# HGRN2's scan: TensorE's work of a head in four groups instead of thirteen steps

## The chip, the core and the metric

The kernel runs on one core of a Trainium2 chip. The metric is the device time of one execution in microseconds (us). A core has five engines that matter here: TensorE (PE; its weight loads are listed as PEld), VectorE (DVE), ScalarE (ACT), GpSimd (POOL) and SyncE (SP, which issues DMAs). Each takes its own queue in order, and semaphores tie the queues together.

## What is computed

One inference step of a decoder with two layers on 512 prompt tokens and 64 sample tokens (8 sequences of 8). The change lies in layer 0's token mixer, HGRN2, a gated linear recurrence with 8 heads of size 128:

```python
q, fz, v, g = jnp.split(x @ w_in, 4, axis=-1)
f = lbf + (1.0 - lbf) * jax.nn.sigmoid(fz)
qh = heads(jax.nn.silu(q) * HG_QK_SCALE)
kh = heads(1.0 - f)
# per token: S_t = diag(f_t) S_{t-1} + k_t v_t^T,  o_t = S_t^T q_t   (computed in chunks)
o, s = hgrn2_chunk_scan(qh, kh, heads(v), heads(jnp.log(f)), s0)
o = rms_norm(o, gnorm_w) * jax.nn.silu(heads(g))
return o.reshape(bsz, t, D_MODEL) @ w_out, s
```

The samples start from a given state per sequence and head, the prompt from zero. Output, new prompt state and new sample states are all results.

## The kernel before

The program is written out by hand: every engine's queue holds its instructions in the order in which the code issues them, and no scheduler moves them. The HGRN2 stage goes head by head. `proj(h)` is a generator that issues the projections of head h and yields after each unit, a unit being three TensorE matmuls into the same output (the activations and the weights are each split into a high and a low part; lines L299 to L301). A head has 16 units for the forget gate f, 16 for q and 16 for the output gate g, each 16 made of 8 with 320 columns and 8 with 256. An even head has 40 units of 256 columns for V ahead of them, for itself and the next head. So an even projection has 88 units and an odd one 48.

Behind each 16 units a side generator is queued, and each unit issues one step of the oldest: `decay` (from f: e, L, k and the four running sums b, on ACT and DVE), `factors` (KH, QH, KL, QL, K2, E2 and the load of the sample states S0) and `queries` (silu of q and g on ACT, tile qg, then QH, QL and Q2 on DVE; it waits QWAIT = 9 steps first).

`scan(h)` is head h's recurrence, a generator whose steps are issued between the units of `proj(h+1)`, at the unit numbers of `SCAN_AT` (the first tuple where the projection is of an even head, the second where it is odd; a step stands behind the unit of its number, the first being number 0). A step ends at each `yield`. What TensorE does in the steps: transposes of K2 (L661, L668), the states (L674 for the prompt, L688 for the samples), the scores of four blocks of 128 tokens (L704, L709, one step per block), products of the samples' queries with their states (L719), the samples' scores (L725), the outputs (L732, L735, L741, L743) and the sum of squares for the norm (L752). DVE makes from them S (the running prompt states), So (new sample states, in two halves), att and ats (scores under a mask, L713 and L727) and the scaled output xf; ACT copies kT, S and oc out of the accumulator banks and computes r. All these matmuls are in plain 32-bit floats, the projections in the split form.

The accumulator memory has eight banks: four with the tag mm for projections, two tr, one o and one os. A tile with a tag that is in use waits for the last reader of the tile before it. Weights stream from memory: SP loads wraw, ACT rounds it to whi, DVE subtracts to wlo, in a ring of five slots of 8 weight blocks.

The last head, 7, has no next projection; its steps are issued between the first units of the output projection (`mix_out`, LAST_AT).

## Time and profile before

| | |
|---|---|
| Median of 3 runs | 1597.84 us (1597.0 to 1600.13) |
| The profiled execution | 1600.95 us, its span 1599.1 us |
| TensorE busy | 1516.2 us, 95% of the span |
| DVE, ACT, POOL busy | 940.2, 687.7, 238.6 us |
| Mean granted TensorE clock | 0.98 |

The HGRN2 stage with its projections lies between about 10 and 340 us of the span. In rows of the timeline the first number is the start in us from the span's start, the second the length in us of the group, then engine, line, operation, out<-in with the program's names, shape and count, and in brackets the idle time ahead of it with what ended it. Rows of matmuls overlap, since they are pipelined: what one costs is read from the start of the next. A row of the waits gives who waited for whom, the total in us, how often, and the longest. A row of the chain of waits gives start, length, engine, tile and line.

### The profile page before, as it was taken

To read this page: it belongs to the slowest core of one execution; us is meant where nothing else is said; L and a number is where in the kernel's file an instruction comes from. 1 tells how busy PE (TensorE), PEld (TensorE's weight loads), DVE (VectorE), ACT (ScalarE), POOL (GpSimd) and SP (SyncE) were. 2 spreads that over 40 slices of the span, in tenths; PEclk is the share of its full clock that TensorE was granted. 3 is DMA by queue.
4 is the path that set the end of the run, shared out by engine and by line. 5 is a ranking of instruction groups with operands and counts; after the bars stand their busy time and mean duration, and the time that the engine had idled before them with its cause. 6 is when DMAs were issued, how large, how long until landed. Compare 5 with 4: busy or idle time off the path is not lost.

```text
span 1599.1 us, 30007 instructions
## 1 busy us (share of the span) xinstructions
PE 1516.2 (95%) x12550; PEld 1468.0 (92%) x12550; DVE 940.2 (59%) x1833; ACT 687.7 (43%) x1159; POOL 238.6 (15%) x284
## 2 busy tenths in 40 slices
PE   8999999889999999999999956799999999999998
PEld 8898989788999999999989956799999999999997
DVE  5748475858557666743486799457533333334685
ACT  5646464736532233123377533336522232133375
POOL 1303020202001112260012432202000000000111
PEclk9999999999999999999999997899999999999999
DMA  5213131242225666753216973332222222223021
GB/s 184 96 67 108 68 109 68 83 126 93 67 70 145 194 191 182 213 153 94 79 67 197 166 280 83 88 106 80 67 80 93 80 80 80 92 80 119 28 79 59
DMA packets 96390, 175.59 MB, mean 110 GB/s; under 512 B 41792, under 2 KB 56816, under 8 KB 96256
## 3 DMA queue, kind: packets, MB, share of 16 engines
q1 hardware_dynamic: 87856, 149.56, 30.7%
q0 software_dynamic: 8400, 24.13, 5.5%
q8 instruction: 98, 1.61, 0.4%
q14 instruction: 36, 0.29, 0.1%
HBM read 148.72 MB, written 24.94 MB: 109 GB/s over the span
## 4 chain that ended last, share of the span: by engine, by line
PE 76%; DVE 14%; ACT 5%; DMA 2%; issue 2%; POOL 1%; SPq 0%; DVEq 0%; ACTq 0%; POOLq 0%
PE mm L299 24%; PE mm L300 23%; PE mm L301 23%; DVE xh L203 2%; DVE wlo L203 1%; DVE xl L203 1%; DVE am L203 1%; DVE b L580 1%; DVE ac L203 1%; DVE xf L203 1%; PE mm L1377 1%; PE tr L709 1%; ACT whi L200 1%; DVE ln_z L203 1%; DVE ln_q L203 1%
## 5 line engine op out<-in xcount | busy, mean ns | idle before, releaser
L299 PE MATMUL mm<-xh,whi 128*128 128x288 f32 x2048 | 611.1, 298 | 7.6 <-ACT xh L200 4.0
L300 PE MATMUL mm<-xl,whi 128*128 128x288 f32 x2048 | 610.2, 298 | 4.5 <-POOL xl L203 3.0
L301 PE MATMUL mm<-xh,wlo 128*128 128x288 f32 x2048 | 607.6, 297 | 1.3 <-DVE wlo L203 1.3
L299 PEld LDWEIGHTS mm<-xh,whi 128*128 128x128 f32 x2048 | 389.0, 190 | 14.0 <-ACT xh L200 5.6
L300 PEld LDWEIGHTS mm<-xl,whi 128*128 128x128 f32 x2048 | 388.9, 190 | 8.1 <-POOL xl L203 4.6
L301 PEld LDWEIGHTS mm<-xh,wlo 128*128 128x128 f32 x2048 | 388.8, 190 | 1.5 <-DVE wlo L203 1.5
L200 ACT ACTIVATE whi<-wraw 128x1024 fp32r<-128x1024 f32 x208 | 218.6, 1053 | 223.1 <-PE mm L300 122.4
L203 DVE TENSOR_TENSOR wlo<-wraw,whi 128x1024 fp32r<-128x1024 f32 x200 | 246.1, 1247 | 29.3 <-ACT whi L200 28.7
L299 PE MATMUL mm<-hhi,whi 128*128 128x288 f32 x704 | 209.6, 298 | 0.0
L301 PE MATMUL mm<-hhi,wlo 128*128 128x288 f32 x704 | 207.8, 295 | 0.0
L300 PE MATMUL mm<-hlo,whi 128*128 128x288 f32 x704 | 207.5, 295 | 0.0
L203 DVE TENSOR_TENSOR fs<-fs,mm 128x288 f32<-128x288 f32 x88 | 40.0, 454 | 267.3 <-PE mm L301 258.2
L299 PEld LDWEIGHTS mm<-hhi,whi 128*128 128x128 f32 x704 | 132.3, 188 | 1.7 <-issue 1.4
L300 PEld LDWEIGHTS mm<-hlo,whi 128*128 128x128 f32 x704 | 132.3, 188 | 0.3
L301 PEld LDWEIGHTS mm<-hhi,wlo 128*128 128x128 f32 x704 | 132.2, 188 | 0.0
L299 PE MATMUL mm<-xhi,whi 128*128 128x320 f32 (+1 forms) x384 | 121.7, 317 | 0.0
L300 PE MATMUL mm<-xlo,whi 128*128 128x320 f32 (+1 forms) x384 | 113.6, 296 | 0.0
L301 PE MATMUL mm<-xhi,wlo 128*128 128x320 f32 (+1 forms) x384 | 113.5, 295 | 0.0
L203 POOL TENSOR_TENSOR ln_s<-ln_s,xf 128x288 f32<-128x288 f32 x24 | 24.3, 1010 | 576.5 <-DVE xf L203 454.9
L200 ACT ACTIVATE hhi<-fs 128x288 fp32r<-128x288 f32 x88 | 38.9, 442 | 149.3 <-DVE fs L203 149.3
L197 ACT ACTIVATE fs<-mm,eps 128x288 f32<-128x288 f32 x88 | 44.1, 501 | 136.0 <-PE mm L301 135.8
L299 PEld LDWEIGHTS mm<-xhi,whi 128*128 128x128 f32 x384 | 72.8, 190 | 6.9 <-issue 4.4
(292 smaller groups left out, 2159.9 us busy)
## 6 DMA issues: line engine op xcount, KB each, us to landing
wraw<-in_w_dram SPq DMA_DIRECT2D x198, 512.0 KB
wraw<-in_w_dram POOLq DMA_DIRECT2D x10, 512.0 KB, 5.2
S<-in_s_dram SPq DMA_DIRECT2D x8, 512.0 KB
out_hgs_dram<-So SPq DMA_DIRECT2D x8, 512.0 KB
wr<-wt_scratch SPq DMA_DIRECT2D x16, 256.0 KB
bT<-in_s5bt_dram SPq DMA_DIRECT2D x16, 256.0 KB
cl_scratch<-cl POOLq DMA_DIRECT2D x16, 256.0 KB, 3.2
zw_scratch<-zw POOLq DMA_DIRECT2D x16, 256.0 KB, 6.2
```

The source lines that it names most:

```text
L197: nc.scalar.activation(out, in_, func, bias=ZERO if bias is None else bias, scale=scale)
L200: nc.scalar.activation(out, in_, ACT.Copy)
L203: (eng or nc.vector).tensor_tensor(out, x, y, op=op)
L299: nc.tensor.matmul(out, whi, rhi, start=start, stop=False)
L300: nc.tensor.matmul(out, whi, rlo, start=False, stop=False)
L301: nc.tensor.matmul(out, wlo, rhi, start=False, stop=stop)
L580: nc.vector.tensor_tensor_scan(b[l], segm[l], L, 0.0, op0=OP.mult, op1=OP.add)
L709: nc.tensor.matmul(ps[s0:s0 + l, o + s0 + l:o + s0 + 2 * l], KL[:, q0:q0 + l], QL[:, q0:q0 + l], start=True, stop=True)
L1377: nc.tensor.matmul(ps[r:r + 64, c], w[:, j, r:r + 64], xo[:, c], start=True, stop=True)
```

## The change

A new generator `grouped_scan(h)` takes the place of `scan(h)` for heads 0 to 6; head 7 keeps `scan`. It has seven steps, at the units of `GROUP_AT`, and TensorE has work in four of them: the transposes, all scores, the samples' scores and their query-state products (first step); prompt and sample states (second); all outputs (fifth); the sums of squares (sixth). The third and fourth are So's halves on DVE, the last the scaled output. The scores of the prompt now go into bank o, the sample scores and the query-state products share a tr bank with the second transpose (ps1), and one half of the sample states goes into bank os instead of an mm bank. Q2 is asked for at the start.

```diff
-SCAN_AT = ((2, 4, 10, 16, 20, 26, 30, 34, 38, 42, 46, 50, 54, 60, 68, 74), (2, 4, 6, 9, 12, 15, 17, 19, 21, 23, 26, 33, 34, 36, 41, 45))
+GROUP_AT = ((15, 24, 28, 32, 40, 48, 54), (14, 20, 23, 26, 31, 36, 41))
...
+        def grouped_scan(h):
...
+            while "Q2" not in d:
+                run(sides.pop(0))
...
+            nc.gpsimd.tensor_tensor(vm[64:128], Vh[64:128, 4:5, :].to_broadcast([64, 4, 128]),
+                                    vmask[64:128, :, None].to_broadcast([64, 4, 128]), op=OP.mult)
...
+            ps, ps1, sc = tr_bank(), tr_bank(), bank("o", 1)
+            for j in range(4):
+                nc.tensor.transpose(ps[:, j * 128:j * 128 + 128], K2[:, j * 128:j * 128 + 128], ident)
+            copy(kT[:, 0:4, :], ps.rearrange("p (j k) -> p j k", j=4))
+            nc.tensor.transpose(ps1[:, 0:128], K2[:, T - 128:T], ident)
+            copy(kT[64:128, 4, :], ps1[64:128, 0:128])
+            for j in range(4):
+                o = j * 128
+                nc.tensor.matmul(sc[:, o:o + 128], KH[:, o:o + 128], QH[:, o:o + 128], start=True, stop=True)
+            for j in range(4):
+                for i, l in LEVELS:
...
+                        nc.tensor.matmul(sc[s0:s0 + l, j * 128 + s0 + l:j * 128 + s0 + 2 * l],
+                                         KL[:, q0:q0 + l], QL[:, q0:q0 + l], start=True, stop=True)
+            att, ats = att_sb[h % 2], ats_sb[h % 2]
+            nc.vector.copy_predicated(att, attm, sc.rearrange("p (j k) -> p j k", j=4))
+            nc.tensor.matmul(ps1[64:128, 128:192], KH[:, NP:T], QH[:, NP:T], start=True, stop=True)
+            nc.vector.copy_predicated(ats[64:128, :], smask[64:128, :], ps1[64:128, 128:192])
+            for q in range(8):
+                c, o = NP + 32 * (q // 4), 256 + 128 * (q // 4)
+                nc.tensor.matmul(ps1[32 * (q % 4):32 * (q % 4) + 32, o:o + 128],
+                                 Q2[:, c:c + 32], S0[:, q, :], start=True, stop=True)
...
+            copy(oc, ps1[:, 256:512].rearrange("p (r v) -> p r v", r=2))
+            yield
+            ps = tr_bank()
...
+            pss = [tr_bank(), bank("os", 1)]
+            for half, p in enumerate(pss):
+                r = slice(64 + 32 * half, 96 + 32 * half)
+                nc.tensor.matmul(p, kT[r, 4, :], vm[r].rearrange("p q v -> p (q v)"), start=True, stop=True)
...
+            nc.sync.dma_start(a["hgp"][h], S[:, 3, :])
+            yield
...
+            for half in (1, 0):
+                for i in range(4):
...
+                        pss[half][:, i * 128:i * 128 + 128], OP.mult, OP.add)
+                yield
+            nc.sync.dma_start(a["hgs"][h], So)
+            ops, ob = bank("os", 1), bank("o", 1)
...
-            at = SCAN_AT[h % 2]
+            at = GROUP_AT[h % 2]
...
-            g = scan(h)
+            g = (scan if h == H - 1 else grouped_scan)(h)
```

DVE's row in an odd projection (here projection 1 with the scan of head 0) reads so before, from the first weight tile behind K2:

```order
L203 TENSOR_TENSOR wlo<-wraw,whi 128x1024 x2
L206 SCALAR_TENSOR_TENSOR S<-S,E_468,tr 128x128 x3
L206 SCALAR_TENSOR_TENSOR So<-S_469,E_468,tr 128x128 x4
L206 SCALAR_TENSOR_TENSOR QH<-qg,QH 128x576
L206 SCALAR_TENSOR_TENSOR QL<-qg,QL 128x256 x3
L206 SCALAR_TENSOR_TENSOR Q_624<-qg,E_468 128x576
L206 SCALAR_TENSOR_TENSOR So<-S_469,E_468,mm 128x128 x4
L568 TENSOR_SCALAR e<-e 128x576
```

and so after (e, L and the b tiles belong to the next head; S_469 is S0):

```order
L795 COPY_PREDICATED ats_149<-msk,tr 64x64
L568 TENSOR_SCALAR e<-e 128x576
L203 TENSOR_TENSOR L<-L,e 128x576
L580 SCALAR_TENSOR_TENSOR b_684<-seg_131,L 128x576
L582 TENSOR_SCALAR k<-k 128x576
L580 SCALAR_TENSOR_TENSOR b_690<-seg_135,L 128x576
L580 SCALAR_TENSOR_TENSOR b_695<-seg_139,L 128x576
L206 SCALAR_TENSOR_TENSOR S<-S,E_468,tr 128x128 x3
L580 SCALAR_TENSOR_TENSOR b_715<-seg_143,L 128x576
L203 TENSOR_TENSOR wlo<-wraw,whi 128x1024
L206 SCALAR_TENSOR_TENSOR So<-S_469,E_468,os 128x128 x4
L206 SCALAR_TENSOR_TENSOR So<-S_469,E_468,tr 128x128 x4
```

S and So stood ahead of QH and of the next head's scans; now they stand behind them and behind a wlo.

ACT's row at the same place, before:

```order
L200 ACTIVATE whi<-wraw 128x1024
L200 ACTIVATE kT<-tr 128x512
L200 ACTIVATE kT<-tr 64x128
L200 ACTIVATE S<-tr 128x128
L200 ACTIVATE qg<-mm 128x320
L200 ACTIVATE qg<-mm 128x256
L197 ACT_TABLE_LOAD
L197 ACTIVATE qg<-qg,eps 128x1152
```

and after:

```order
L200 ACTIVATE qg<-mm 128x320
L200 ACTIVATE qg<-mm 128x256
L197 ACT_TABLE_LOAD
L197 ACTIVATE qg<-qg,eps 128x1152
L641 ACT_TABLE_LOAD
L200 ACTIVATE kT<-tr 128x512
L200 ACTIVATE kT<-tr 64x128
L200 ACTIVATE oc<-tr 128x256
```

The copies of kT and S moved from ahead of qg to behind it.

TensorE's row at the outputs of head 0, with the semaphores that an instruction waits for, before (the block of sample outputs, two steps with projections between):

```order
L732 MATMUL os<-msk,oc 128x32 [waits DMAHW2_49]
L732 MATMUL os<-msk,oc 128x32
L299 MATMUL mm<-xhi,whi 128x320
L300 MATMUL mm<-xlo,whi 128x320
L301 MATMUL mm<-xhi,wlo 128x320
L735 MATMUL os<-ats_149,V 128x64 [waits DVE_49]
```

and after:

```order
L829 MATMUL os<-msk,oc 128x32 [waits DMAHW2_49,DVE_49,PE_49]
L829 MATMUL os<-msk,oc 128x32
L831 MATMUL os<-ats_149,V 128x64
L835 MATMUL o<-att_147,V 128x128 x2
L837 MATMUL o<-Q_592,S 128x128 [waits Activation_49]
```

The outputs stand together, and the first of them waits for DVE, which reads So from bank os.

## The prediction

> **What bounds the kernel now.** First the page: who is busy, and which engine carries the chain that ended last.

> ```profile
> PE 1516.2 (95%) x12550; PEld 1468.0 (92%) x12550; DVE 940.2 (59%) x1833; ACT 687.7 (43%) x1159; POOL 238.6 (15%) x284
> PE 76%; DVE 14%; ACT 5%; DMA 2%; issue 2%; POOL 1%; SPq 0%; DVEq 0%; ACTq 0%; POOLq 0%
> ```

> TensorE bounds the kernel, but 19% of the chain lies on DVE and ACT. Then the waits of TensorE in the HGRN2 stage (27 to 345 us), and the rows of two of them:

> ```profile
> PE tr L661 <- DVE K L203: 8.7, 4, 3.3
> ...
> 47.65 1.11 PE L661 MATMUL tr<-cst,K 128*128 128x128 f32 x4 [3.30 <-DVE K L203]
> ...
> 127.27 0.66 PE L661 MATMUL tr<-cst,K 128*128 128x128 f32 x4 [1.79 <-DVE K L203]
> ```

> TensorE stands still once in each odd projection, for K2. Nothing else in the seven inner heads costs it over 0.5 us. So the stage is TensorE's work plus four short stalls, and the change is worth what it takes from the work, less the stalls that it makes.

> The timeline of TensorE prices the work. "Unit" means a projection's three matmuls; steps of the scan stand between units.

> ```profile
> 108.77 0.31 PE L299 MATMUL mm<-xhi,whi 128*128 128x320 f32 x1
> ...
> 109.21 0.31 PE L299 MATMUL mm<-xhi,whi 128*128 128x320 f32 x1
> ...
> 110.97 0.61 PE L741 MATMUL o<-att,V 128*128 128x128 f32 x4
> ...
> 112.45 0.39 PE L299 MATMUL mm<-xhi,whi 128*128 128x320 f32 x1
> ...
> 115.62 1.13 PE L752 MATMUL tr<-sq,ones 128*128 128x288 f32 x4
> 116.38 0.49 PE L299 MATMUL mm<-xhi,whi 128*128 128x256 f32 x1
> ...
> 156.75 0.29 PE L299 MATMUL mm<-whi,xhi 128*128 128x256 f32 x1
> ...
> 173.18 0.28 PE L299 MATMUL mm<-whi,xhi 128*128 128x256 f32 x1
> ...
> 173.54 0.38 PE L704 MATMUL tr<-QH,KH 128*128 128x128 f32 x2
> 173.85 0.56 PE L709 MATMUL tr<-QL,KL 128*16 128x16 f32 x14
> 174.34 0.39 PE L299 MATMUL mm<-whi,xhi 128*128 128x256 f32 x1
> ...
> 185.73 0.31 PE L299 MATMUL mm<-xhi,whi 128*128 128x320 f32 x1
> ```

> A unit of 320 columns takes 0.44 us (108.77 to 109.21), one of 256 0.355. A score step takes 0.80 (173.54 to 174.34), and the next matmul starts about 0.1 late. I call 108.77 time 0: the f units of head 2 end and its q units begin. The next projection (head 4, even) begins at 156.75, time 47.98; its f units end at 185.73, time 76.96. That is one pair of heads.

> **Work removed.** From 156.75 to 185.73, 28.98 us, run 56 units (48 at 0.355, 8 at 0.44: 20.5) and eleven steps of head 3: 8.5. Its last two take 1.5 (110.97 to 112.45) and 0.97 (L752: 0.76 and a late start). A head's scan costs 11.0.

> In groups: transposes 5 x 0.11 = 0.55; first group's rest, scores 4 x 0.22 and 4 x 0.47 (the L709 row: 14 passes in 0.49), sample scores and query-states, 3.6; the state group as the last head runs it today, back to back, 314.37 to 316.52 with a late start, 2.25; the output group 1.5 + 0.85; the norm group 0.97. Sum 9.7: 1.3 saved a head, 9 us over seven. Its bounds: nine returns fewer at 0.1 is 0.9 a head, and at twice that 1.8.

> ```profile
> 314.37 1.16 PE L674 MATMUL tr<-V,kT 128*128 128x128 f32 x8 [1.17 <-ACT kT L200]
> ...
> 316.52 0.40 PE L299 MATMUL mm<-xh,whi 128*128 128x288 f32 x1
> ```

> **Wait A: QH in an odd projection.** The chain of waits, ACT's and DVE's rows behind time 0:

> ```profile
> 122.06 0.74 DVE r L206
> ...
> 123.72 1.61 DVE K L203 x2
> 125.35 0.78 ACT K L197
> ...
> 128.85 0.87 ACT L200 ACTIVATE kT<-tr 128x512 f32<-128x512 f32 x2
> ...
> 130.90 0.71 ACT L200 ACTIVATE qg<-mm 128x320 f32<-128x320 f32 x2
> ...
> 134.21 0.76 DVE QH L206
> ```

> In the new order the previous head's r and xf are finished before time 0, so K moves up by 1.66 and ACT's K exponent starts at 123.7. The kT and S copies no longer stand ahead of qg, which starts 3.5 later (125.35 to 128.85): 127.2. QH starts 3.3 after qg (130.90 to 134.21) and ends at 131.25, time 22.5. TensorE is there after 32 units (12.7), 15 more (6.0) and the transposes: time 19.25. K2 is ready by then, so its stall of 1.8 goes; the stall for QH that comes is 3.3. In the order before, L704 needed QH at unit 15 too, but 4.7 us of steps lay ahead of it. Bounds: 1.8 (K2's stall keeps its size) to 4.0.

> **Wait inside the first group.** The sample scores and the query-state products share bank ps1, and the built program lets L798 wait for DVE's copy ats, which stands behind att, which needs the last L790.

> ```profile
> 147.09 0.74 DVE L713 COPY_PREDICATED att<-msk,tr 128x512 f32<-128x512 uint32 x1
> 147.86 0.23 DVE L727 COPY_PREDICATED ats<-msk,tr 64x64 f32<-64x64 uint32 x1
> ```

> 0.74 + 0.23 and two hand-overs: 1.1 a head, for which nothing else is queued on TensorE. Bounds 0 and 1.3. The group ends at time 22.5 + 3.6 + 1.1 = 27.2.

> **Wait B: bank os in an odd projection.** This is the largest term. L829 writes bank os, where L810 put half of the sample states, and waits until DVE has read them (So). DVE's row has So behind the next head's e, L, four scans of b and a wlo. Rows for that chain:

> ```profile
> 108.86 1.06 ACT whi L200
> ...
> 136.45 0.88 ACT L197 ACTIVATE e<-mm,eps 128x320 f32<-128x320 f32 x2
> ...
> 131.03 1.11 DVE L206 SCALAR_TENSOR_TENSOR S<-S,E,tr 128x128 f32<-128x128 f32 x3 [0.70 <-ACT S L200]
> 132.93 1.12 DVE L206 SCALAR_TENSOR_TENSOR So<-S,E,tr 128x128 f32<-128x128 f32 x4 [0.78 <-PE mm L688]
> ...
> 145.97 1.20 DVE L203 TENSOR_TENSOR wlo<-wraw,whi 128x1024 fp32r<-128x1024 f32 x1
> ```

> The f units end one unit after the first group (27.55); whi starts then (at 108.86 it started with the end of the f units too), e at 28.65. From e's start to wlo's end is 147.17 - 136.45 = 10.7 today; S and So add 2.2: So is read at 41.55. TensorE arrives after 6 units (2.55), the state group (2.25) and 11 units (4.15): 36.15. Stall 5.4, bounds 4 and 7. Then output group 2.35, 5 units 2.2, norm group 0.97, 11 units 4.15: the odd projection ends at 51.2, against 47.98: +3.2.

> **Even projections.** So stands ahead of the scans there; no wait B. Wait A: QH hangs on the V copy ahead of qg.

> ```profile
> 160.31 0.38 ACT L200 ACTIVATE V<-mm 128x256 f32<-128x256 f32 x1 [0.79 <-PE mm L301]
> ...
> 163.90 0.76 DVE L206 SCALAR_TENSOR_TENSOR QH<-qg,QH 128x576 f32<-128x576 f32 x1 [4.04 <-ACT qg L197]
> ```

> V is done 8 units in (2.85, copied from 3.0), QH ends 3.6 + 0.75 later: 7.35. TensorE is there at 16 x 0.355 + 0.55 = 6.2: stall 1.15. Group 4.7, 9 units 3.2, 2.25, 16 units 5.75, 2.35, 8 units 3.45, 0.97, 7 units 2.5: 32.4 against 28.98, of which 2.5 are head 3's last two steps moved ahead of time 0. So +3.4; a pair costs +6.6.

> Four odd and three even projections: 4 x 3.2 + 3 x 3.4 = 23. Projection 1 stalls 3.30 already and lost some of its clock: -1. The last head keeps its order, and the norm of head 6 is done five units sooner, which frees ACT for its splits: -1. Sum +21. The moved output DMAs of S and So sit on SP's queue ahead of weight loads; wlo ran in time behind a five-slot ring, and I cost them nothing; without that cover a late load shows as a wait for whi.

> **The clock.** The stage view with the granted clock (the third column from the end):

> ```profile
> 46.53:53.36 6.83, 5.71 (x24) 5.67 (x25) 4.41 (x3) 3.29 (x7) 5.23 (x4) 0.50 0.41 128
> 125.05:128.45 3.40, 1.60 (x12) 1.34 (x12) 2.56 (x3) 3.10 (x6) 2.99 (x4) 1.00 0.00 0
> ```

> The idle 3.30 before 47.65 brought 6.83 us at half clock; the idle 1.79 before 127.27 none. Waits A (3.3) and B (5.4) lie on the 3.30's side. Each at half clock for 3.4 to 6.8 us loses 1.7 to 3.4 of work; behind A only what falls into the first group counts, since B's slack takes the rest. I take 1.2 for A and 1.9 for B: 12.4 over four odd projections. Bounds 0 and 27.

> [...]

> **Sum.** 21 + 12.4 = 33.5. The profiled execution took 1600.95 (span 1599.1): 1634.5. The median of the runs is 1597.84, 3.1 lower: 1631.

> **Rivals.** (1) The waits come and the clock holds: +21, 1619. For it: the 1.79 row; against it: the 3.30 row. [...] Chance 0.22. (2) Faster: DVE runs ahead of TensorE in the odd projections, so that neither A nor B binds. It is one mechanism, on DVE's queue: its chain behind time 0 would have to be 3.3 us shorter, the one behind the f units 5.4 us. For it: DVE is busy 59%; against it: both chains are made of rows that wait for each other, and their 22.5 and 12.9 us are read off rows as they run today. Then 9 of work and 8.7 of old stalls (3.30, and 1.79 three times) go, 7.7 (ats) and 3.5 (even projections) come: 1591. It decides at a chain of 7.5 us from e to So. Chance of a faster kernel 0.04, of one within 0.2% (3.2 us, about what a measurement here can tell from no change) 0.03. (3) B is half as long, if DVE's scans and wlo find fewer gaps than today: +21 - 11 + 8, 1616; against it: DVE takes its queue in order, and wlo ends 10.7 behind e today. Chance 0.08. (4) Longer half-clock stretches, 6.8 us behind each wait: 21 + 25, 1644. Chance 0.13. The forecast itself, 1624 to 1638: 0.5.

> **How the numbers follow.** The likeliest case gives 1631. Down to 1610 the range takes rival 1, rival 3 and waits a microsecond shorter each; up to 1645 it takes rival 4. What is left out is 0.07 for faster or same and a little beyond each end. Slower 0.93, same 0.03, faster 0.04.

> **What would show it.** In the changed trace: no wait of L778 for K; waits of L784 for QH of about 3.3 in odd and 1.1 in even projections; L798 about 1.1 behind L790; L829 waiting 5 to 6 us for DVE So, four times; So behind wlo in DVE's rows; a granted clock of 0.5 after L829. A head's TensorE work should read 9.7 without the waits. The prediction is wrong if L829 waits less than 2 us, or if the first group waits for nothing.

## The result and the profile after

| | median, us | against before |
|---|---|---|
| before, in the same comparison | 1598.78 (1597.0 to 1600.13) | |
| after | 1645.24 (1642.85 to 1646.06) | 1.0286, interval 1.027 to 1.0302 |

Below, "before" and "after" stand for the two kernels. The change costs 46 us. 1631 was forecast, and the time lies at the upper end of the range, where rival 4 stood (1644, longer stretches at half clock). The profiled execution took 1646.01 us, its span 1644.2. The page's lines on the engines and on the chain that ended last:

```profile
PE 1531.7 (93%) x12550; PEld 1486.1 (90%) x12550; DVE 936.1 (57%) x1833; ACT 687.8 (42%) x1159; POOL 243.1 (15%) x284
PE 72%; DVE 16%; ACT 7%; issue 2%; DMA 2%; POOL 0%; SPq 0%; DVEq 0%; ACTq 0%; POOLq 0%
```

The same 12550 matmuls keep TensorE busy for 15.5 us longer than before (1516.2), so waits alone cannot be the cause: work has become slower. The waits of TensorE between 27 and 385 us:

```profile
PE o L784 <- DVE QH L206: 15.6, 7, 3.5
PE os L829 <- DVE So L206: 12.5, 3, 4.2
PE tr L798 <- DVE ats L795: 7.6, 7, 1.1
PE os L829 <- issue: 4.3, 1, 4.3
```

All three forecast waits are there (the row put down to "issue" is the first wait of L829). No L778 waits for K. One pair of heads, an even and an odd projection in the steady part of the stage, shows the split. Columns: the stretch, its length, busy time of PE, PEld, DVE, ACT and POOL with counts, granted clock, DMA share, GB/s. First before, from one first transpose (L661) to that of two heads later:

```profile
80.83:157.80 76.97, 75.08 (x657) 68.77 (x656) 49.41 (x80) 43.81 (x72) 12.49 (x10) 1.00 0.25 85
```

and after, from L778 to L778:

```profile
182.04:270.77 88.73, 78.39 (x656) 73.08 (x655) 48.01 (x80) 43.82 (x72) 14.12 (x10) 0.90 0.22 74
```

A pair takes 11.76 us more. TensorE stands idle for 88.73 - 78.39 = 10.34 us in it, against 1.89 before: 8.45 more. It is busy 3.31 us longer although the groups hold less work, because the granted clock is 0.90: 88.73 x 0.10 x 2, some 17 us of a pair, ran at half clock, and none before. A table in steps of the clock shows where. In this profile's record of the clock the 17 stretches at half clock begin at multiples of 3.4133 us from each other, to within 2 ns, so the windows of this table lie on that grid. Wait A (139.8 to 142.6) and wait B (160.0 to 164.2) of one odd projection after:

```profile
135.51:138.93 3.42, 3.42 (x29) 3.42 (x28) 3.25 (x3) 3.42 (x8) 3.42 (x4) 1.00 0.17 71
138.93:142.34 3.41, 0.85 (x8) 0.61 (x6) 2.15 (x3) 3.36 (x4) 2.28 (x2) 1.00 0.57 172
142.34:145.75 3.41, 3.20 (x36) 2.76 (x36) 1.74 (x5) 1.45 (x3) 0.00 (x0) 0.50 0.36 141
145.75:149.17 3.42, 2.35 (x44) 1.76 (x47) 0.95 (x2) 0.00 (x0) 0.00 (x0) 0.50 0.00 0
149.17:152.58 3.41, 3.41 (x24) 3.03 (x16) 0.30 (x1) 2.22 (x4) 0.00 (x0) 0.50 0.00 0
152.58:155.99 3.41, 3.41 (x22) 2.53 (x22) 1.63 (x3) 2.30 (x3) 0.00 (x0) 1.00 0.00 0
...
159.40:162.82 3.42, 0.64 (x6) 0.43 (x4) 3.32 (x6) 0.00 (x0) 0.00 (x0) 1.00 0.08 22
162.82:166.23 3.41, 2.02 (x8) 1.87 (x9) 3.41 (x13) 0.31 (x1) 0.00 (x0) 0.50 0.55 186
166.23:169.65 3.42, 3.42 (x17) 3.42 (x17) 1.35 (x4) 0.47 (x1) 0.00 (x0) 0.50 0.77 274
```

A window in which TensorE is idle for 2.56 of 3.41 us (138.93) is followed by windows at half clock. Behind A there are three of them, 10.24 us: the second holds the wait for ats, is idle for 1.07 us, and the clock does not come back after it. Behind B there are two.

Three of DVE's rows of the same odd projection show what the two waits waited for:

```profile
141.65 0.76 DVE L206 SCALAR_TENSOR_TENSOR QH<-qg,QH 128x576 f32<-128x576 f32 x1 [1.26 <-ACT qg L197]
161.83 1.20 DVE L203 TENSOR_TENSOR wlo<-wraw,whi 128x1024 fp32r<-128x1024 f32 x1
162.95 1.12 DVE L206 SCALAR_TENSOR_TENSOR So<-S,E,os 128x128 f32<-128x128 f32 x4
```

Time 0 of the prediction's walk lies at 120.39 here. QH ended at time 22.0, where 22.5 was forecast, and TensorE came to it at 19.4, where 19.25 was forecast; before, QH ended at 26.2. DVE had read the half of So in bank os at time 43.7 (41.55 forecast), and TensorE came to L829 at 39.65 (36.15 forecast).

### The profile page after: what moved, and what is told of

Same layout as the page of the kernel before. It is cut to its first block, busy times and chain, and to the rows that moved or that the text cites. A ratio compares the mean times of both kernels' runs of the same rounds, so it can differ in the third digit from the quotient of the medians.

```text
span 1644.2 us, 30049 instructions
## 1 busy us (share of the span) xinstructions
PE 1531.7 (93%) x12550; PEld 1486.1 (90%) x12550; DVE 936.1 (57%) x1833; ACT 687.8 (42%) x1159; POOL 243.1 (15%) x284
## 3 DMA queue, kind: packets, MB, share of 16 engines
q8 instruction: 98, 1.61, 0.4%
## 4 chain that ended last, share of the span: by engine, by line
PE 72%; DVE 16%; ACT 7%; issue 2%; DMA 2%; POOL 0%; SPq 0%; DVEq 0%; ACTq 0%; POOLq 0%
PE mm L299 22%; PE mm L300 22%; PE mm L301 21%; DVE xh L203 2%; DVE b L580 2%; DVE wlo L203 1%; ACT whi L200 1%; DVE ac L203 1%; DVE xl L203 1%; DVE am L203 1%; PE o L790 1%; DVE xf L203 1%; DMA wraw<-in_w_dram 1%; PE o L835 1%; ACT e L197 1%
## 5 line engine op out<-in xcount | busy, mean ns | idle before, releaser
L299 PE MATMUL mm<-xh,whi 128*128 128x288 f32 x2048 | 611.1, 298 | 8.6 <-ACT xh L200 5.5
L301 PE MATMUL mm<-xh,wlo 128*128 128x288 f32 x2048 | 607.7, 297 | 2.3 <-DVE wlo L203 2.3
L299 PEld LDWEIGHTS mm<-xh,whi 128*128 128x128 f32 x2048 | 389.2, 190 | 15.4 <-ACT xh L200 6.6
L301 PEld LDWEIGHTS mm<-xh,wlo 128*128 128x128 f32 x2048 | 389.0, 190 | 2.5 <-DVE wlo L203 2.5
L200 ACT ACTIVATE whi<-wraw 128x1024 fp32r<-128x1024 f32 x208 | 218.6, 1053 | 205.2 <-PE mm L300 101.4
L203 DVE TENSOR_TENSOR wlo<-wraw,whi 128x1024 fp32r<-128x1024 f32 x200 | 247.0, 1251 | 48.8 <-ACT whi L200 48.3
L299 PE MATMUL mm<-hhi,whi 128*128 128x288 f32 x704 | 209.6, 298 | 0.0
L301 PE MATMUL mm<-hhi,wlo 128*128 128x288 f32 x704 | 207.7, 295 | 0.0
L203 DVE TENSOR_TENSOR fs<-fs,mm 128x288 f32<-128x288 f32 x88 | 40.0, 454 | 270.2 <-PE mm L301 261.2
L299 PEld LDWEIGHTS mm<-hhi,whi 128*128 128x128 f32 x704 | 132.3, 188 | 1.7 <-issue 1.4
L301 PEld LDWEIGHTS mm<-hhi,wlo 128*128 128x128 f32 x704 | 132.2, 188 | 0.0
L299 PE MATMUL mm<-xhi,whi 128*128 128x320 f32 (+1 forms) x384 | 119.3, 311 | 0.0
L301 PE MATMUL mm<-xhi,wlo 128*128 128x320 f32 (+1 forms) x384 | 115.0, 300 | 0.0
L203 POOL TENSOR_TENSOR ln_s<-ln_s,xf 128x288 f32<-128x288 f32 x24 | 24.2, 1010 | 574.4 <-DVE xf L203 454.3
L197 ACT ACTIVATE fs<-mm,eps 128x288 f32<-128x288 f32 x88 | 44.1, 501 | 139.3 <-PE mm L301 139.3
L200 ACT ACTIVATE hhi<-fs 128x288 fp32r<-128x288 f32 x88 | 38.9, 442 | 150.6 <-DVE fs L203 150.6
L299 PEld LDWEIGHTS mm<-xhi,whi 128*128 128x128 f32 x384 | 75.3, 196 | 4.9 <-issue 4.6
```

The source lines that it names most:

```text
L197: nc.scalar.activation(out, in_, func, bias=ZERO if bias is None else bias, scale=scale)
L200: nc.scalar.activation(out, in_, ACT.Copy)
L203: (eng or nc.vector).tensor_tensor(out, x, y, op=op)
L299: nc.tensor.matmul(out, whi, rhi, start=start, stop=False)
L301: nc.tensor.matmul(out, wlo, rhi, start=False, stop=stop)
```

## The experiments

The theory: the loss is the three waits plus the half clock that waits A and B bring; each wait is made by one thing (QH late in the queue, bank ps1, bank os). The main rival: the half clock comes from the groups themselves, or a wait that is taken away comes back elsewhere. The ratios are those to the kernel before on the same chip; a difference in ratio is turned into us with 1598.

### Wait B's bank

```diff
-            pss = [tr_bank(), bank("os", 1)]
+            pss = [tr_bank(), mm_bank()]
```

> The changed kernel, but the second half of the samples' states goes into a bank of the projections' own instead of bank os, so that L829 no longer needs a bank that So must leave first. Theory (wait B is a wait for the bank, and its idle TensorE brings the half clock behind it): the four waits of 4.2 us (16.8 us) go, and the four stretches of 6.83 us at half clock behind them go too (about 2.7 us each, 10.8 us): 1645 - 27.6 = about 1618 us. Rival 1 (the half clock does not come from the idle time): only the waits go, about 1628 us, and stretches at half clock remain near L829. Rival 2 (VectorE is late with whatever comes next, the state S or the projections' bank): a new wait of 3 us or more stands near L829 or at the projections' first matmul, and the time stays at 1635 us or above.

Measured: 1619.05 us, ratio 1.0146 (1.0128 to 1.0163). That is 26 us less than after by the medians and 22 by the ratios, near the theory's 27.6 and above rival 1's 17. Waits between 86 and 310 us:

```profile
PE o L784 <- DVE QH L206: 12.5, 6, 2.8
PE tr L798 <- DVE ats L795: 6.4, 6, 1.1
PE tr L847 <- DVE So L206: 0.5, 1, 0.5
```

and one pair:

```profile
166.78:247.82 81.04, 74.34 (x656) 69.05 (x655) 48.59 (x80) 43.61 (x72) 14.72 (x10) 0.96 0.24 81
```

L829's wait is gone, and the clock of the pair rises to 0.96 (0.94 in the pair ahead of it). A small part returned: L847 waits in three of four odd projections, up to 1.1 us, for So's half in the tr bank. So wait B was the bank, as the order of DVE's row had it. That the gain comes so near the theory's is in part luck. The shorter pair (81.04 us, 23.7 windows) meets the grid at other points, and behind A the four odd projections have 20.5 us at half clock together, against 37.6 after, which the theory did not have.

### The samples' scores in another bank

```diff
-            nc.tensor.matmul(ps1[64:128, 128:192], KH[:, NP:T], QH[:, NP:T], start=True, stop=True)
-            nc.vector.copy_predicated(ats[64:128, :], smask[64:128, :], ps1[64:128, 128:192])
+            ps3 = bank("os", 1)
+            nc.tensor.matmul(ps3[64:128, 128:192], KH[:, NP:T], QH[:, NP:T], start=True, stop=True)
+            nc.vector.copy_predicated(ats[64:128, :], smask[64:128, :], ps3[64:128, 128:192])
```

> The changed kernel, but the samples' scores go into bank os instead of the bank that holds the fifth transpose, so that L798 no longer waits for VectorE's ats. Theory: the seven waits of 1.07 us inside the first group go and nothing takes their place before the waits for QH and So, which are measured from VectorE's side: in odd projections VectorE decides when So is done, so there up to 1.07 us of each gain comes back as a longer wait at L829; in even ones the gain is whole. 1645 - 7.5 = about 1637 us if it is whole everywhere, about 1641 us if only three even heads gain it. Rival: VectorE's queue decides everywhere (the transposes' evictions and the states wait for it), and the time stays within 1 us of 1645 us.

Measured: 1634.58 us, ratio 1.0236 (1.022 to 1.0251): 8 to 11 us less than after, where 4 or 7.5 were expected. In the waits between 86 and 310 us the row of ats is gone, and those of QH and So read as after:

```profile
PE o L784 <- DVE QH L206: 9.3, 5, 2.8
PE os L830 <- DVE So L206: 8.3, 2, 4.2
```

```profile
92.70:178.10 85.40, 77.25 (x654) 72.19 (x654) 48.03 (x80) 43.82 (x72) 14.12 (x10) 0.92 0.23 76
```

The pair is 3.33 us shorter, but only 2.19 of that is idle time (8.15 against 10.34). The rest is the clock (0.92 against 0.90, 13.7 us at half clock against 17): the stretch behind A is one window shorter in the last three odd projections, where no wait for ats stands any more. In the first it is one window longer (10.24 against 6.83), behind a wait for QH of 4.3 us. My caution that B would grow by what ats gave back was wrong: B stayed at 4.2.

### Both banks

> The changed kernel with both bank edits: the samples' scores in bank os, the second half of the states in a bank of the projections' own. Theory: with L829 free of So the 1.07 us of L798 is gained in every head: 1618 - 7.5 = about 1610 us, which is what is left of the change beside the wait for QH (A, 4 x 2.8 to 3.5 us, with its four stretches of 10.24 us at half clock, about 4.5 us each) and the even projections' 1.26 us. Rival: gains do not add, since VectorE is behind in its queue: 1618 us or above.

Measured: 1612.04 us, ratio 1.0094 (1.0067 to 1.012), 31 to 33 us less than after. The gains add. What is left against before is wait A with its clock and the even projections' wait for QH; waits between 86 and 310 us:

```profile
PE o L784 <- DVE QH L206: 12.5, 6, 2.8
PE tr L848 <- DVE So L206: 1.1, 1, 1.1
```

### Is it TensorE's idleness that halves the clock?

Work is added and none is taken away, so that TensorE is busy in waits A and B; what the added matmuls write is overwritten.

```diff
+FILL = (24, 40)
...
+            if h % 2 == 0:
+                for n in range(FILL[0]):
+                    nc.tensor.matmul(sc[:, 0:256], xhih[:, 0, 0:128], xhih[:, 1, 0:256], start=True, stop=True)
...
+            if h % 2 == 0:
+                for n in range(FILL[1]):
+                    nc.tensor.matmul(ob[:, 0:256], xhih[:, 0, 0:128], xhih[:, 1, 0:256], start=True, stop=True)
```

> The changed kernel with work added and nothing taken away: ahead of L784 24 and ahead of L829 40 matmuls of 128 x 256 on data that is always there, for the even heads only (their groups lie in the odd projections); what they write is overwritten. TensorE is then busy where it stood idle in waits A and B. Theory (the half clock comes from TensorE standing idle there): the stretches of 10.24 and 6.83 us go, which cost about 4.5 and 2.7 us an odd projection, near 24 to 28 us in all; the added matmuls take about the time that the waits took (24 and 40 at about 0.11 us are 2.6 and 4.4 us): about 1621 us, faster though it does more. Rival (the half clock comes from something else in these groups, such as their small matmuls or the long run of evictions): the stretches stay, and the time is 1645 us or more. If the clock falls only later, the time lies between.

Measured: 1628.32 us, ratio 1.0194 (1.0177 to 1.0211): 15 to 17 us less than after with 256 more matmuls. The theory had about 1621, the rival 1645 or more. The gain tells against the rival: the groups and their small matmuls are unchanged. Two pairs:

```profile
88.50:172.07 83.57, 79.73 (x720) 75.23 (x719) 47.99 (x80) 43.84 (x72) 14.13 (x10) 1.00 0.23 78
172.07:258.09 86.02, 82.62 (x720) 78.09 (x719) 48.00 (x80) 43.84 (x72) 14.13 (x10) 0.96 0.23 76
```

The first ran wholly at full clock and is 5.2 us shorter than after's. The second shows why the gain stayed below the 24 us expected: two windows at half clock remain (0.04 x 86.02 x 2 = 6.9 us), although A and B are filled. The window ahead of one of them, and that one:

```profile
175.80:179.21 3.41, 2.34 (x59) 1.76 (x52) 0.95 (x2) 0.28 (x1) 0.00 (x0) 1.00 0.02 5
179.21:182.62 3.41, 3.41 (x18) 3.41 (x17) 0.00 (x0) 0.38 (x2) 0.00 (x0) 0.50 0.00 0
```

TensorE was idle there for 1.07 us only, the wait for ats. What stood ahead of that wait in this window are small matmuls:

```profile
175.10 1.98 PE L794 MATMUL o<-QL,KL 128*16 128x16 f32 x55
176.82 0.27 PE L798 MATMUL tr<-QH,KH 128*64 128x64 f32 x1
...
178.22 0.65 PE L802 MATMUL tr<-S,Q 128*32 128x128 f32 x16 [1.07 <-DVE ats L799]
```

So the rival may be right in part: in this window 1.07 us of idle time behind small matmuls was followed by half clock (0.50 at 179.21). To tell whether the small matmuls are enough by themselves, the two edits were put together, both fills and the samples' scores in bank os:

> The kernel with both fills, and the samples' scores in bank os, so that TensorE is busy in waits A and B and does not wait for ats. In the run with both fills some half clock was left, and each stretch followed a window of the clock in which TensorE was idle for only 1.07 us (the wait for ats) and had the small matmuls of L794 ahead of it. Theory (a window of small matmuls counts as half idle, so that 1.07 us more are enough; small matmuls alone are not): with the ats wait gone no window at half clock stands between 80 and 310 us, each pair takes 83.57 - 2.14 = 81.4 us at a granted clock of 1.00, and the time is 1628 - 7.5 - some 5 = about 1616 us. Rival 1 (small matmuls alone lower the clock): stretches remain and the time is about 1621 us. Rival 2 (the 1.26 us wait for QH in even projections was the cause): stretches remain in the even projections, about 1621 us.

Measured: 1617.88 us, ratio 1.0126 (1.0105 to 1.0147), 10 to 11 us less than with the fills alone. Two pairs:

```profile
86.53:167.93 81.40, 79.71 (x721) 75.35 (x720) 48.04 (x80) 43.85 (x72) 14.13 (x10) 1.00 0.24 80
167.93:249.22 81.29, 79.60 (x721) 75.24 (x720) 48.04 (x80) 43.83 (x72) 14.12 (x10) 1.00 0.24 81
```

81.4 us at full clock were expected, and 81.3 to 81.4 came. The small matmuls are all still there, and so is the 1.26 us wait in even projections; without the wait for ats the clock is 1.00 through both pairs. The total alone would not tell theory (1616) from rivals (1621); the clock in the trace does.

### Which of the two waits pays more

Each fill by itself: first ahead of L784 only, `FILL = (24, 0)`, then ahead of L829 only, `FILL = (0, 40)`.

> The changed kernel with only the 24 added matmuls ahead of L784 for the even heads, so TensorE is busy in wait A and stands idle in wait B as before. Theory (a clock stretch behind A costs only what B's slack does not take): the first group runs at full clock and ends about 3.3 us sooner, TensorE comes to L829 sooner and the idle there grows from 4.2 to about 5.4 us or more, so of the 4.5 us an odd projection only about 1.2 us come back: 1645 - 5 = about 1640 us. Rival (VectorE's end of So moves up with the first group, so B does not grow): 1645 - 18 = about 1627 us, as in the run with both fills.

Measured: 1632.54 us, ratio 1.0212 (1.0198 to 1.0226): 12 to 13 us less than after, between the theory's 5 and the rival's 18. The waits of L836 (L829 before the added lines) between 86 and 310 us:

```profile
PE os L836 <- DVE So L207: 10.5, 2, 5.2
```

B grew from 4.17 to 5.2 us there; in the other two odd projections it read 4.3 and 4.2. So A's stretch costs about 3 us an odd projection (12 / 4) after what B gives back.

> The changed kernel with only the 40 added matmuls ahead of L829 for the even heads, so TensorE is busy in wait B. Theory: the four stretches at half clock behind L829 (6.83 us each) go and those behind A (10.24 us) stay: 2.7 us an odd projection, 1645 - 11 = about 1634 us, less what the added matmuls take beyond the wait (up to 1 us each): 1634 to 1638 us. Rival (the stretch behind B is a late effect of A): the stretches stay, 1645 us or more.

Measured: 1636.54 us, ratio 1.0232 (1.0217 to 1.0247): 9 us less than after, 2.2 an odd projection, within the theory's 1634 to 1638. B's stretches are gone, as it had it (the clock of its two pairs is 0.96 and 0.94, where after's are 0.90). A's did not all stay: they are 10.24, 3.41, 10.24 and 10.24 us, and a new one of 3.41 stands behind a wait for ats at 97.9. So the 3 and the 2.2 are what each edit paid in all, with what changed in the other stretches.

### What does grouping save by itself?

The kernel before, with the units of the four score steps made equal, so that these stand together:

```diff
-SCAN_AT = ((2, 4, 10, 16, 20, 26, 30, 34, 38, 42, ...), (2, 4, 6, 9, 12, 15, 17, 19, 21, 23, ...))
+SCAN_AT = ((2, 4, 10, 16, 20, 38, 38, 38, 38, 42, ...), (2, 4, 6, 9, 12, 21, 21, 21, 21, 23, ...))
```

> The kernel before with one edit: the four score steps of a head stand at one place (unit 38 in even, 21 in odd projections) instead of four. No bank, no wait and no order on the other engines is meant to change. Theory (bringing TensorE's steps together saves about 0.1 us at each return to the projections' matmuls, which the changed kernel hides under its waits): three places fewer a head, 7 heads, 2 to 5 us: 1592 to 1595 us against 1597. Rival (grouping saves nothing by itself): within 1 us of 1597 us. Rival 2 (att is later and L732 waits for it): slower than 1598 us.

Measured: 1598.43 us, ratio 0.9999 (0.9989 to 1.0008). Nothing was saved, as the first rival had it, and the timeline of TensorE says why:

```profile
173.28 0.38 PE L704 MATMUL tr<-QH,KH 128*128 128x128 f32 x2
173.60 0.56 PE L709 MATMUL tr<-QL,KL 128*16 128x16 f32 x14
174.09 0.49 PE L704 MATMUL tr<-QH,KH 128*128 128x128 f32 x2
...
176.33 0.56 PE L709 MATMUL tr<-QL,KL 128*16 128x16 f32 x14
176.82 0.38 PE L299 MATMUL mm<-whi,xhi 128*128 128x256 f32 x1
```

Four blocks back to back take 3.54 us from the first L704 to L299, and a block repeats every 0.81 to 0.91 us. Before, a step by itself took 0.80. I read it so: at a change between the 128 x 128 matmuls of L704 and the small ones of L709 TensorE loses about as much as at a return to the projections. That is an estimate from these rows. So in the next kernel the eight matmuls of L704 go first, then the 56 small ones, for heads 0 to 6, at that same place:

```diff
             for j in range(4):
                 nc.tensor.matmul(ps[:, o:o + 128], KH[:, o:o + 128], QH[:, o:o + 128], start=True, stop=True)
-                for i, l in LEVELS:
+                for jj in (range(4) if j == 3 and h < H - 1 else [j] if h == H - 1 else []):
+                    for i, l in LEVELS:
```

> The kernel before with the scores of heads 0 to 6 at one place, and there all eight 128 x 128 matmuls of L704 first and then the 56 small ones of L709; in the run with the four blocks at one place these alternated four times, and nothing was saved. Theory (TensorE loses about 0.25 us at each change between whole-array and small matmuls, not at the return to the projections): three such alternations fewer, 0.75 us a head, 5 us over seven heads: about 1593 us against 1598. Rival (the changed kernel's saved microsecond a head comes from the samples' scores and queries standing among the scores): nothing is saved here, 1597 to 1599 us.

```profile
173.10 1.05 PE L704 MATMUL tr<-QH,KH 128*128 128x128 f32 x8
174.09 2.04 PE L711 MATMUL tr<-QL,KL 128*16 128x16 f32 x56
176.06 0.38 PE L299 MATMUL mm<-whi,xhi 128*128 128x256 f32 x1
```

Now the scores take 2.96 us instead of 3.54: 0.6 a head is saved, of the 0.75 expected, and in the trace a pair of heads takes 75.8 to 76.4 us from L661 to L661, where it took 77.0 before. The time did not show it: 1599.21 us, ratio 1.0 (0.9989 to 1.001), the rival's figure and not the theory's 1593. L737 now waits 0.53 us for ats in each odd projection, which takes part of it back; the other 2 us are about what the interval cannot tell.

The changed kernel had already that order, and more. Its first group in an even projection:

```profile
184.01 1.13 PE L784 MATMUL o<-QH,KH 128*128 128x128 f32 x8 [1.26 <-DVE QH L206]
185.07 1.98 PE L790 MATMUL o<-QL,KL 128*16 128x16 f32 x55
...
188.19 0.64 PE L798 MATMUL tr<-S,Q 128*32 128x128 f32 x16 [1.07 <-DVE ats L795]
188.76 0.39 PE L299 MATMUL mm<-whi,xhi 128*128 128x256 f32 x1
```

188.76 - 184.01 - 1.07 = 3.68 us for all scores, the samples' scores and the query-states. Against the sorted scores alone the samples' part adds 0.7.

### The same groups, cut where the data is ready

If the waits are the whole loss, groups without them must be faster than before. This order has the transposes by themselves, then states with S and So behind them at once, then all scores (the samples' in bank os, the query-states in a tr bank of their own), outputs and norm. In odd projections the side steps pause for four units, so that att stands ahead of the next head's e in DVE's queue. The edit is to the changed kernel; the reordered steps of `grouped_scan` are left out here.

```diff
-GROUP_AT = ((15, 24, 28, 32, 40, 48, 54), (14, 20, 23, 26, 31, 36, 41))
+GROUP_AT = ((8, 14, 16, 22, 40, 48, 54), (8, 14, 15, 19, 33, 38, 43))
+HOLD = (16, 19)
...
-                if n % SIDE == 0 and sides and not step(sides[0]):
+                if not (h % 2 and HOLD[0] <= n <= HOLD[1]) and sides and not step(sides[0]):
```

> Groups again, but cut where the data is ready: transposes first, then states with S and So at once (in the tr banks and a bank of the projections' own), then all scores with the samples' scores in bank os, then outputs, norm and the scaled output; in odd projections the side steps pause for units 16 to 19, so that att stands ahead of the next head's e on VectorE. Theory (the loss lay in the waits for QH, ats and So and in the half clock that they brought, not in the grouping): none of these waits is left over 0.5 us, no stretch at half clock stands in the odd projections, and the grouping's own 1 us a head is left as a gain, with the old stalls for K2 (3.3 and three of 1.8) gone: 1578 to 1590 us. Rival (each early group finds another late operand: kT, S or the projections' bank): a wait of over 1 us in each projection, 1597 us or above.

Measured: 1593.81 us, ratio 0.9964 (0.9951 to 0.9978), faster than before but short of the theory's 1578 to 1590. In heads 0 to 6 the waits for QH, ats, So and K (but for one of 0.9 us) are gone, yet a new one stood in each odd projection, for sq; the first of the waits between 27 and 310 us:

```profile
PE tr L849 <- ACT sq L198: 11.1, 4, 2.8
```

ACT computes sq behind the next head's KH, and KH waits for DVE's scans. So I moved outputs and norm ahead of KH, and the states by one unit, for a wait of 0.48 us for vm:

```diff
-GROUP_AT = ((8, 14, 16, 22, 40, 48, 54), (8, 14, 15, 19, 33, 38, 43))
-HOLD = (16, 19)
+GROUP_AT = ((8, 14, 16, 22, 40, 48, 54), (8, 15, 16, 20, 27, 31, 41))
+HOLD = (16, 20)
```

> The five-group order with the odd projections' units changed, after the profile of the run before: the outputs at unit 27 and the norm at 31, ahead of the next head's KH on ScalarE (there sq stood behind KH, which waited for VectorE, and L849 waited 2.77 us in each odd projection), states at unit 15 (L787 waited 0.48 us for vm), scores at 20, side steps paused from 16 to 20. Theory: both waits go and nothing takes their place: 4 x 2.77 + 4 x 0.48 = 13 us off 1594, 1579 to 1584 us. Rival (the odd projection's end then runs into K of the next transposes, whose chain on VectorE does not get shorter): a wait for K of 2 to 3 us at L775, 1590 us or above.

Measured: 1580.67 us, ratio 0.9885 (0.9868 to 0.9903): 18 us faster than before, 65 faster than the changed kernel and within the theory's 1579 to 1584. Its pair:

```profile
77.15:148.86 71.71, 71.59 (x656) 67.45 (x655) 48.22 (x81) 44.06 (x72) 14.62 (x11) 1.00 0.27 91
```

TensorE is idle for 0.12 us of 71.71. Against before, 1.77 us of idle time and 3.49 us of work are gone in a pair. Grouping paid here, where every operand was ready.

## Why the prediction was right, and where its size was off

The direction, the three waits, their places and what each waited for were right. The sizes, in us for a pair of heads in the steady part:

| step | predicted | measured |
|---|---|---|
| wait A, L784 for QH, odd | 3.3 | 2.77 |
| wait in the first group, L798 for ats | 2 x 1.1 | 2 x 1.07 |
| wait B, L829 for So | 5.4 | 4.17 |
| wait A, even | 1.15 | 1.26 |
| old stall for K2 | -1.8 | -1.8 |
| half clock behind A and B | 1.2 + 1.9 | about 6.4 |
| pair, all together | 9.7 | 11.76 |

**Waits and work.** Over the stage the four rows of waits sum to 40.0 us, and the old stalls of 8.7 are gone: 31.3 more idle time, where the terms put 37.3. (Over the whole program it is 45.1 - 15.5 = 29.6; in the last head a wait for QH shrank from 2.7 to 0.2.) In a pair idle time gives +8.45, and the rest of its 11.76, 3.31, is work and clock together. I split it so: the pair of the last kernel above is 71.6 us of busy time at full clock, and its groups hold nearly what the changed kernel's hold (an estimate of 72.0 for those, from their even groups); before it was 75.1. The run with both fills and the bank agrees: its pair is 79.65 at full clock, and without 64 added matmuls of 0.118 (a third of a unit of 0.355) that is an estimated 72.1. So some 3.1 are saved a pair, 1.5 a head, against 1.3 predicted, or 11 us over seven heads. 31.3 - 11 = +20, and +21 was the forecast's sum without the clock. That these agree is partly luck: the waits were smaller, and the saving was larger than the 1.3, which the walk along the units had partly in it (its terms for the even projections add up to 32.5, not 32.4). My reason for the saving was only half of it. Standing together saved nothing by itself: a block of scores repeated every 0.81 to 0.91 us in a row, where a step alone took 0.80. Sorting the scores by form gives 0.6 of the 1.5; no run takes the rest apart.

**The clock** is the term that was mis-sized: 12.4, where 45.1 (the difference of the spans) - 20 leaves some 25, near the upper bound of 27; a pair gives 3.31 + 3.1, about 6.4. The clock's own record agrees. Between 27 and 385 us 75.1 us ran at half clock, against 10.2 before, and TensorE was busy for 63.0 of them, against 9.1. Half of the difference, 27 us, is the most that can be lost by it. One of the stretches (357.4 to 367.6) belongs to the last head, for which the forecast had no term. That the clock loss follows the waits was right: with A and B filled the first pair ran at 1.00, with B alone filled B's stretches were gone. B's share was about right: 1.9 predicted, 2.2 measured with the fill. A's share was 1.2 predicted, 3 measured. (TensorE's busy time in a stretch, halved, gives at most 4.5 behind A and 2.7 behind B.) I took 3.4 to 6.8 us at half clock behind each wait; behind A it lasted 10.24. The window rows show what lay in it: the first group's small matmuls and the wait for ats fall into the stretch (1.07 us idle in the window of 145.75, the clock 0.50 in it and in the next), and where ats did not wait, the stretch was a window shorter in three of four. I had priced A and ats apart, and here they fell into one stretch. I had also let B's slack take what is lost behind the first group; B gave back 1.07 us at most, and in only two of four odd projections.

**Wait B** was 1.2 smaller than predicted, since TensorE came 3.5 later than the walk had it and So only 2.1 later. With A filled, so that the clock did not fall behind it, it read 5.2 in two odd projections, close to the 5.4.

**The rivals.** Rival 1 (the clock holds) and rival 3 (B half as long) are out. Rival 2 (DVE ahead) never came near: the waits for QH were 2.77 in three odd projections and 3.45 in the first. Rival 4 gave 1644 for 6.8 us behind each wait; measured were 10.24 and 6.83 behind the two, and the time was 1645. The covers that I costed at nothing, the moved DMAs on SP's queue and the weight loads, held: no row of the waits names a weight tile in heads 1 to 6.

## What to carry to other kernels

Grouping TensorE's work paid here only as far as every operand and every bank was ready where the group stood (18 us faster than before, against 46 slower); look in the other engines' queues for what stands ahead of each operand, and cut the groups there. Price waits that stand close to each other together: here the 1.07 us for ats began 4.9 us behind the end of the 2.77 us for QH, and the clock was 0.50 for 10.24 us from the end of the first on. When work is grouped, try it sorted by form: that took the scores from 3.54 to 2.96 us a head here (too little for the total to show), and standing together alone took nothing from them.

## What the runs showed of the hardware

**The same wait, at two places of the grid.** The same idle time of 2.77 us brought 10.24 us at half clock in the profile after, and none in one odd projection of the first five-group kernel. There the wait (148.1 to 150.8) lay across two windows of the grid:

```profile
145.67:149.09 3.42, 2.39 (x17) 2.13 (x15) 3.42 (x5) 0.00 (x0) 0.00 (x0) 1.00 0.44 173
149.09:152.50 3.41, 1.66 (x9) 1.46 (x10) 1.85 (x6) 3.27 (x6) 2.23 (x2) 1.00 0.00 0
152.50:155.91 3.41, 3.41 (x32) 3.41 (x31) 2.44 (x2) 3.38 (x8) 3.41 (x3) 1.00 0.00 0
```

**The same short wait, behind different work.** The window of 175.80 in the kernel with both fills holds the 1.07 us wait for ats and 2.34 us of work, and half clock followed (0.50 at 179.21). Three windows of after, in its even projections (97.96, 186.71 and 275.46), hold the same 1.07 us and the same 2.34 us of work at full clock, and the clock of the next window is 1.00. They differ in where the 55 small matmuls ahead of the wait lay: 1.3 of their 1.98 us in the window of 175.80, 0.3 to 0.5 us in those of after, the rest in the window before. With the small matmuls and no wait for ats (both fills and the bank) the clock was 1.00 in both pairs. That the small matmuls are the reason is my reading of these places; no run shows it apart from the wait.

**After's pair stays in step with the grid.** It takes 88.73 us, 26 windows (88.75), so wait A meets the grid at nearly the same point each time in the last three odd projections (0.25, 0.24, 0.24 of a window), and 10.24 us at half clock followed each time. The pair with the samples' scores in another bank takes 85.40, 25 windows (85.33). Whether the length of a pair is drawn to the grid or met it by chance is not shown.
